# A two-layer hybrid encoder on one core: the beginning written out by hand, two DMA queues at both ends

## The chip, the core and the metric

The kernel runs on one NeuronCore of a Trainium2 chip. The core has TensorE (matrix products and transposes, into PSUM), VectorE, ScalarE (ACT in the profile) and GpSimd (POOL) for everything else, and SyncE (SP), which here only issues transfers. Each engine works through its own instructions in program order and waits on semaphores for the others; sixteen DMA engines move data between HBM and SBUF. The metric is the device time in microseconds of one execution, as the median over several runs.

## What is computed

The reference is a trunk of DEPTH = 2 layers over x of 256 tokens by 1024 channels, all in float32:

```python
h = rms_norm(x, norm_mix_g)
proj = h @ w_in                       # 1024 x 2304, split into nine parts of 256
# four branches: retention, pooling, neighbourhood attention, memory attention
up = jnp.einsum('bsnc,ncd->bsnd', branches, w_branch)
gates = jax.nn.sigmoid(h @ w_gate).reshape(b, s, N_BRANCH, dm)
x = x + jnp.einsum('bsnd,bsnd->bsd', gates, up) @ w_out
a, g = jnp.split(rms_norm(x, norm_ffn_g) @ w_ffn_in, 2, axis=-1)
x = x + (jax.nn.silu(a) * g) @ w_ffn_out
```

The products with the weights (w_in, w_gate, w_mem_kv, w_branch, w_out, w_ffn_in, w_ffn_out) are nearly all of the arithmetic.

## The kernel before

The 256 tokens are two tiles of 128, t = 0 and 1. The weights come in 272 *slots* of 128 x 1024 numbers (two rows of 128 input channels by 512 output channels, as a rule), in the order in which TensorE takes them. A slot is loaded into one of four buffers `raw` by a DMA (512 KB), and then split: ScalarE copies it, rounded to float32r, to `whi` (`split_hi`, line 272), and VectorE writes the rest, `raw - whi`, to `wlo` (`split_lo`, line 277). `split_lo` also calls `issue_dmas` (line 260), which has SP issue the loads of the slots whose buffers come free. The activations are split in the same way into hi and lo. One product of 128 x 128 by 128 x 512 is made of three: hi with `whi`, hi with `wlo`, lo with `whi`. A slot gives each token tile two such triples (`emit`, six products of TensorE), so both tiles take twelve.

Before the first product, x must be there with the channels on the partitions. Each half (512 channels) of each tile is transposed in four blocks by TensorE against an identity matrix, into a PSUM bank; ScalarE scales by the norm's gain and rounds to `hhi`, VectorE writes `hlo` (`half_norm`). What scales by the RMS comes after the products.

The order of all instructions is found while the program is built. A class `Clock` keeps an estimate in microseconds of when each engine gets to what it has been given. The main loop (from line 1020) lets the chains of small work go on whose operands should be there (`background`), splits weights when the engines have caught up (`pump`), and then emits the next slot of one of the tiles. For the beginning this means: SP issues all first loads, in the order x of tile 0 first half, identity with gains, slot 0, x of tile 1 first half, slot 1, the two second halves of x, slots 2 and 3 (lines 1003 to 1010); four chains `half_norm` wait for their halves of x; and while the estimate says that the first slot isn't ready, the loop gives TensorE products of zeros (`B<-w` in the profile), which keep it busy. At the end, `store` adds the last product to x in pieces of 256 columns and has SP issue a DMA for each.

Of the kernel before, what the change touches and what calls it, by code (L numbers as in the profile page):

```python
# [42 lines left out]
class Engine:  # L43
    """An engine of nc whose instructions are also entered in the clock."""
# [19 lines left out]
class Clock:  # L64
    """An estimate in microseconds of when each engine gets to what has been given to it:
    the small work is handed out when its operands should be there, so that no queue waits on it."""
# [81 lines left out]
def tile_encoder(ctx: ExitStack, tc: tile.TileContext, a: dict, out: bass.AP):  # L148
# [103 lines left out]
    state = {"dma": 0, "hi": 0, "lo": 0, "free": 0, "urgent": 0}  # L252
# [7 lines left out]
    def issue_dmas(n=NR):  # L260
        while state["dma"] < min(n_slots, state["lo"] + n):
            j = state["dma"]
            src, dims = slots[j]
            dst = shaped(RAW[j % NR], dims)
            if len(dims) == 2:
                nc.sync.dma_start(out=dst, in_=src)
            else:
                for k in range(dims[0]):
                    nc.sync.dma_start(out=dst[:, k], in_=src[:, k])
            state["dma"] += 1  # L270

    def split_hi():
        j = state["hi"]
        nc.scalar.copy(WHI[j % NS], RAW[j % NR])
        state["hi"] += 1
# [11 lines left out]
    def pump():  # L287
        """split weights when the engines have caught up, the sooner the fewer slots are ready"""
        window = WINDOW[max(0, min(state["lo"] - items[min(pos[0], len(items) - 1)]["j"], len(WINDOW) - 1))]
        if state["urgent"]:  # L290
            window = min(window, 0.8)
        for _ in range(2):
            j = state["lo"]
            if j < state["hi"] and soon(clock.at["DVE"], window) and soon(clock.last(clock.writes, WHI[j % NS])):
                split_lo()
            j = state["hi"]
            if (j < min(n_slots, state["free"] + NS, state["lo"] + NR) and soon(clock.at["ACT"], window)
                    and soon(clock.last(clock.writes, RAW[j % NR]))
                    and soon(max(clock.last(clock.reads, w[j % NS]) for w in (WHI, WLO)))):
                split_hi()  # L300
# [31 lines left out]
    def start(gen, *reads):  # L332
        """reads: PSUM banks that gen still reads, until it calls done()"""
        hold(*reads)
        chains.append([clock.now, gen])

    def until(step):
        """a chain goes on after what it has just given out (None), that much later (a number), or at a time"""
        return step[0] if isinstance(step, tuple) else clock.mark + (step or 0)

    def background():
        """let every chain go on whose last instructions should be through"""
# [39 lines left out]
    def scale_rows(out, in_, col):  # L382
        """out = in_ * col, on the engine that is free sooner"""
# [6 lines left out]
    def hi_lo(hi, lo, ps, bank, flag):  # L390
        """hi now, lo when hi is there, which ends the hold on bank"""
# [14 lines left out]
    def half_norm(src, t, c, act, gain, flag, bank, pre=None):  # L406
        """Half c of src (token-major) transposed, times gain (there a column), and split.
        What follows the products with it scales by one over the RMS (rms_chain)."""
# [22 lines left out]
    def rms_chain(src, rs, junk, flag, after=()):  # L431
        """rs = one over the RMS of each row of src"""
# [11 lines left out]
    def norm(t, flag, gain, rs, pre):  # L444
        """both halves of the norm of X[t]"""
# [7 lines left out]
    def head_norm(ps, dst, g, scale=None):  # L453
        """dst = ps (times scale, by row) scaled to unit RMS in groups of 64, g of them."""
# [78 lines left out]
    def to_heads(left, right, gains):  # L533
        """Token-major [tok, 256], both, to heads with the token in the free dimension, split for scores left^T right:
        LS has hi of a head on its 64 partitions and lo on the others, RS hi on both, and RL lo."""
# [36 lines left out]
    def scores(out, h, tok):  # L572
        """the scores of head h, for the tokens tok of left, with all of right"""
# [5 lines left out]
    def attention(l, v, branch, bias):  # L579
        """softmax(q k + bias) v for four heads, two at a time, to BHI/BLO[branch]."""  # L580
# [122 lines left out]
    def decay_chain(l):  # L703
        """exp(|i - j| log gamma): the lesser of d lg_fwd and -d lg_bwd, both of which are at most 0 on their side"""
# [17 lines left out]
    def prefetch_chain(l):  # L722
        """parameters, and what comes in once the layer's norms are through"""
# [33 lines left out]
    def log_sigmoid():  # L757
        """lg = log sigmoid of the 16 decays: min(x, 0) - log1p(exp(-|x|))."""
# [27 lines left out]
    def add(n_js, act, bank, nk, n=512, first=True, last=True, req=None, end=None, lag=1):  # L786
        """bank(t) (+)= act of tile t @ the weights of the next n_js slots; nk k-tiles.
        req: what has to be there; end(t): what follows; lag: slots by which tile 0 may lead here."""
# [53 lines left out]
    def hid_chain(l, j, t, ps):  # L842
        """silu(a) * g, token-major"""
# [19 lines left out]
    def store(t, blk):  # L863
        for c in range(blk * 512, blk * 512 + 512, 256):
            o = X[t][:, c:c + 256]
            nc.vector.tensor_add(o, o, A[2 * t + blk][:, c % 512:c % 512 + 256])
            nc.sync.dma_start(out=out[0, t * P:(t + 1) * P, c:c + 256], in_=o)

    def layer(l):
# [23 lines left out]
        for n, br in enumerate(BRANCHES):  # L893
            for blk in range(2):
# [3 lines left out]
                # the gates of the first branch lie around the memory's product  # L898
# [49 lines left out]
    def ready(t):  # L948
        """when the next slot of tile t can be taken"""
# [34 lines left out]
    def warm(*aps):  # L984
        """products of zeros, which keep TensorE at its full clock until aps are there"""
        while clock.now < max(clock.last(clock.writes, x) for x in aps):
            nc.tensor.matmul(B[0][:, 0:P], W[0][:, 0:P], W[0][:, P:2 * P], start=True, stop=True)
            clock.at["PE"] += 0.21 if clock.now < 6.2 else 0
# [6 lines left out]
    with tc.manual_schedule():  # L995
        nc.vector.memset(W[0][:, 0:P], 0.0)
        nc.vector.memset(mhalf, -0.5)
        def load_x(t, c):
            nc.sync.dma_start(out=X[t][:, HALVES[c]], in_=a["x"][0, t * P:(t + 1) * P, HALVES[c]])

        nc.scalar.activation(small[0], mhalf, AF.Square)
        clock.at["ACT"] += 1.2
        load_x(0, 0)
        nc.sync.dma_start(out=ident_gain, in_=a["ident_gain"])
        issue_dmas(1)
        load_x(1, 0)
        issue_dmas(2)
        load_x(0, 1)
        load_x(1, 1)
        issue_dmas()  # L1010
        for c in range(2):
            for t in range(NT):
                start(half_norm(X[t], t, c, act_h, GAIN[0][0], f"h{t}@0", (C[0], B[1], C[1], A[3])[2 * t + c]))
# [5 lines left out]
        assert base[0] == n_slots  # L1019
        while pos[1] < len(items) or chains:  # L1020
# [13 lines left out]
            else:  # L1034
                if pos[0] == 0:
                    nc.tensor.matmul(B[0][:, 0:P], W[0][:, 0:P], W[0][:, 0:P], start=True, stop=True)
                    continue
# [79 lines left out]
```

## Time and profile before

| | |
|---|---|
| median of 3 runs | 852.66 us |
| lowest, highest run | 850.24, 854.39 us |
| span of the profiled execution, first to last instruction | 850.4 us |
| that execution's own time | not recorded beside its span |
| TensorE (PE) busy | 840.0 us, 99% |
| VectorE (DVE), ScalarE (ACT) busy | 553.3 us, 469.6 us |
| moved by DMA | 152.86 MB, mean 180 GB/s |
| mean granted TensorE clock | 0.998 |

In the profile's lines a piece of work is named by its engine, its line and the tiles it writes and reads, out<-in. All instructions go through one helper, so nearly all have line L59 and are told apart by tiles: `hhi`, `hlo` are the activations of the first products, `whi`, `wlo` the split weights, `raw` the loaded ones, A, B and C banks of PSUM. The start of an instruction is in us from the start of the span. PE's busy time counts each product from its start to its modelled end, so two that follow one another overlap: a product of 512 columns shows 0.39 us and the next begins some 0.23 us after it. PEclk is the share of the full clock that TensorE was granted.

### The profile page before, as it was taken

Reading aid. Unit: us, or ns where it says so; the run is one execution under the profiler, and the core shown is the slowest. Engines: PE = TensorE matmul, PEld = TensorE weight load, DVE = VectorE, ACT = ScalarE, POOL = GpSimd, SP = SyncE. Lnnn points to the kernel's source line nnn. Section 1 sums busy time; section 2 is a strip of 40 time slices with the busy share of each in tenths; the row PEclk is TensorE's granted clock in tenths of the full one; section 3 lists DMA queues with packets and bytes.
Section 4 is the critical chain, followed back from the end, with each engine's and each line's share of the span. In section 5 each row is a group of like instructions: output and inputs, shape, how many; then the busy total and the mean of one; then the engine's idle time right before and its main releaser. Section 6 shows DMA issues by size and latency. Waiting matters only on the chain.

```text
span 850.4 us, 10796 instructions
## 1 busy us (share of the span) xinstructions
PE 840.0 (99%) x3934; PEld 678.6 (80%) x3934; DVE 553.3 (65%) x807; ACT 469.6 (55%) x722; POOL 28.6 (3%) x30
## 2 busy tenths in 40 slices
PE   8999999999999999999999999999999999999998
PEld 7887777778887888888888877777788878888886
DVE  5898776665667656555568778567665775665541
ACT  7867867444556444444469676664454654444430
POOL 0300100000000000000012001000000000000000
PEclk9999999999999999999999999999999999999999
DMA  8946764454558666665363567345554675656611
GB/s 267 315 131 202 246 201 132 131 191 160 191 169 259 188 196 187 186 188 186 96 218 121 173 216 250 134 124 182 165 170 131 190 252 183 190 181 192 193 53 50
DMA packets 103749, 152.86 MB, mean 180 GB/s; under 512 B 6416, under 2 KB 55312, under 8 KB 103696
## 3 DMA queue, kind: packets, MB, share of 16 engines
q1 hardware_dynamic: 103696, 152.17, 56.3%
q8 instruction: 31, 0.51, 0.2%
q14 instruction: 22, 0.18, 0.1%
HBM read 151.10 MB, written 1.05 MB: 179 GB/s over the span
## 4 chain that ended last, share of the span: by engine, by line
PE 94%; DMA 3%; DVE 1%; ACT 1%; SPq 0%; issue 0%; DVEq 0%; ACTq 0%
PE A L59 62%; PE B L59 27%; PE C L59 5%; DMA raw<-in_w_ffn_out 2%; DMA mem<-in_pool_a 1%; DVE wlo L59 1%; DMA x<-in_x 1%; ACT whi L59 1%; DVE w L59 0%; SPq L59 0%; DVE x L59 0%; DVEq L1113 0%; ACTq L59 0%
## 5 line engine op out<-in xcount | busy, mean ns | idle before, releaser
L59 DVE TENSOR_TENSOR wlo<-raw,whi 128x1024 fp32r<-128x1024 f32 (+1 forms) x275 | 329.9, 1211 | 183.6 <-ACT whi L59 182.7
L59 ACT CAST whi<-raw 128x1024 fp32r<-128x1024 f32 x272 | 284.3, 1051 | 221.2 <-PE A L59 102.1
L59 PE MATMUL A<-whi,hhi 128*128 128x512 f32 (+1 forms) x544 | 215.6, 396 | 0.1
L59 PE MATMUL A<-whi,hlo 128*128 128x512 f32 (+1 forms) x544 | 209.4, 385 | 0.0
L59 PE MATMUL A<-wlo,hhi 128*128 128x512 f32 (+1 forms) x544 | 209.0, 384 | 0.0
L59 PEld LDWEIGHTS A<-whi,hhi 128*128 128x128 f32 x544 | 102.4, 188 | 24.1 <-issue 5.5
L59 PEld LDWEIGHTS A<-whi,hlo 128*128 128x128 f32 x544 | 102.4, 188 | 21.2 <-DVE hlo L59 0.5
L59 PEld LDWEIGHTS A<-wlo,hhi 128*128 128x128 f32 x544 | 102.6, 189 | 17.9
L59 PE MATMUL B<-whi,hlo 128*128 128x512 f32 x288 | 112.3, 390 | 0.1
L59 PE MATMUL B<-whi,hhi 128*128 128x512 f32 x288 | 112.3, 390 | 0.0
L59 PE MATMUL B<-wlo,hhi 128*128 128x512 f32 x288 | 112.1, 389 | 0.0
L59 PE MATMUL A<-whi,bhi 128*128 128x512 f32 x272 | 109.2, 401 | 0.0
L59 PE MATMUL A<-whi,blo 128*128 128x512 f32 x272 | 106.3, 391 | 0.0
L59 PE MATMUL A<-wlo,bhi 128*128 128x512 f32 x272 | 106.1, 390 | 0.0
L59 PEld LDWEIGHTS B<-whi,hlo 128*128 128x128 f32 x288 | 54.0, 188 | 12.1 <-DVE hlo L59 0.9
L59 PEld LDWEIGHTS B<-wlo,hhi 128*128 128x128 f32 x288 | 54.1, 188 | 11.2
L59 PEld LDWEIGHTS B<-whi,hhi 128*128 128x128 f32 x288 | 54.1, 188 | 11.1
L59 PEld LDWEIGHTS A<-whi,bhi 128*128 128x128 f32 x272 | 51.1, 188 | 11.4 <-issue 0.8
L59 PEld LDWEIGHTS A<-whi,blo 128*128 128x128 f32 x272 | 51.0, 188 | 11.0
L59 PEld LDWEIGHTS A<-wlo,bhi 128*128 128x128 f32 x272 | 51.2, 188 | 9.7
L59 DVE SCALAR_TENSOR_TENSOR w<-B,rms,w 128x256 f32<-128x256 f32 x72 | 34.6, 482 | 3.9 <-ACT w L59 2.6
L59 ACT CAST bhi<-C 128x512 fp32r<-128x512 f32 x28 | 16.4, 587 | 35.2 <-PE C L59 35.1
(112 smaller groups left out, 614.9 us busy)
## 6 DMA issues: line engine op xcount, KB each, us to landing
raw<-in_w_ffn_in SPq DMA_DIRECT2D x176, 256.0 KB, 3.3
raw<-in_w_gate SPq DMA_DIRECT2D x64, 512.0 KB, 3.8
raw<-in_w_ffn_out SPq DMA_DIRECT2D x44, 512.0 KB, 4.0
raw<-in_w_in SPq DMA_DIRECT2D x36, 512.0 KB, 4.6
raw<-in_w_branch SPq DMA_DIRECT2D x16, 512.0 KB, 5.0
raw<-in_w_out SPq DMA_DIRECT2D x16, 512.0 KB, 4.1
raw<-in_w_mem_kv SPq DMA_DIRECT2D x8, 512.0 KB, 5.1
xn<-in_bias SPq DMA_DIRECT2D x4, 512.0 KB, 5.8
```

What stands on the lines that cost most here:

```text
L59: return f(*args, **kw)
```

## The change

Comments and document strings are taken out. Beyond that there are three parts.

The loads of the beginning: ScalarE's queue issues the identity with the gains and the first half of x of tile 1; SP's queue issues the first half of x of tile 0, slot 0 as two transfers of half a slot, slot 1, the second half of x of tile 0, slot 2, the second half of x of tile 1, slot 3.

The beginning of the program: a function `begin` gives out the first instructions in a fixed order, up to the split of slot 3, and the main loop goes on from there. While it runs, `pump` does nothing. x's first halves are handled in pairs of blocks with PSUM banks of their own, the second halves as four blocks. Slot 0 is rounded by ScalarE in two halves. Fifteen products of zeros stand at fixed places. The chains `half_norm` for the first norm are gone.

The end: of the two pieces of each store, the second is issued by ScalarE's queue.

```diff
-            if len(dims) == 2:
+            if len(dims) == 2 and j:
                 nc.sync.dma_start(out=dst, in_=src)
             else:
                 for k in range(dims[0]):
     def split_hi():
         j = state["hi"]
-        nc.scalar.copy(WHI[j % NS], RAW[j % NR])
+        for o in HALVES if j < 1 else [slice(None)]:
+            nc.scalar.copy(WHI[j % NS][:, o], RAW[j % NR][:, o])
...
+        if state["by_hand"]:
+            return
...
     def store(t, blk):
-        for c in range(blk * 512, blk * 512 + 512, 256):
+        for i, c in enumerate(range(blk * 512, blk * 512 + 512, 256)):
             o = X[t][:, c:c + 256]
             nc.vector.tensor_add(o, o, A[2 * t + blk][:, c % 512:c % 512 + 256])
-            nc.sync.dma_start(out=out[0, t * P:(t + 1) * P, c:c + 256], in_=o)
+            (nc.scalar if i else nc.sync).dma_start(out=out[0, t * P:(t + 1) * P, c:c + 256], in_=o)
...
+    def warm(n):
+
+        for _ in range(n):
+            nc.tensor.matmul(B[0][:, 0:P], W[0][:, 0:P], W[0][:, 0:P], start=True, stop=True)
+
+    def begin():
+
+        parts = {(0, 0): (C[0], (0, 1)), (0, 1): (B[1], (2, 3)), (1, 0): (C[1], (0, 1)), (1, 1): (A[3], (2, 3)),
+                 (0, 2): (C[0], (4, 5, 6, 7)), (1, 2): (C[1], (4, 5, 6, 7))}
+
+        def turn(t, *which):
+            for c in which:
+                bank, ks = parts[t, c]
+                for i, k in enumerate(ks):
+                    nc.tensor.transpose(bank[:, i * P:(i + 1) * P], X[t][:, k * P:(k + 1) * P], ident)
+
+        def split(t, c):
+            bank, ks = parts[t, c]
+            ks = [(bank[:, i * P:(i + 1) * P], GAIN[0][0][:, k:k + 1], *act_h(t, k)) for i, k in enumerate(ks)]
+            for ps, g, hi, lo in ks:
+                nc.scalar.activation(hi, ps, AF.Copy, scale=g)
+            for ps, g, hi, lo in ks:
+                nc.vector.scalar_tensor_tensor(out=lo, in0=ps, scalar=g, in1=hi.bitcast(F32), op0=ALU.mult, op1=ALU.subtract)
+            if c:
+                raise_flag(f"h{t}@0c{c - 1}")
+
+        def weights():
+            split_hi()
+            split_lo()
+
+        state["by_hand"] = True
+        warm(10)
+        turn(0, 0, 1)
+        warm(3)
+        split(0, 0)
+        weights()
+        turn(1, 0, 1)
+        warm(2)
+        split(1, 0)
+        emit(0)
+        split(0, 1)
+        emit(1)
+        weights()
+        split(1, 1)
+        turn(0, 2)
+        emit(0)
+        emit(1)
+        split(0, 2)
+        weights()
+        turn(1, 2)
+        split(1, 2)
+        weights()
+        state["by_hand"] = False
...
-        nc.scalar.activation(small[0], mhalf, AF.Square)
-        clock.at["ACT"] += 1.2
-        load_x(0, 0)
-        nc.sync.dma_start(out=ident_gain, in_=a["ident_gain"])
-        issue_dmas(1)
-        load_x(1, 0)
-        issue_dmas(2)
-        load_x(0, 1)
-        load_x(1, 1)
-        issue_dmas()
-        for c in range(2):
-            for t in range(NT):
-                start(half_norm(X[t], t, c, act_h, GAIN[0][0], f"h{t}@0", (C[0], B[1], C[1], A[3])[2 * t + c]))
+        nc.scalar.dma_start(out=ident_gain, in_=a["ident_gain"])
+        load_x(nc.sync, 0, 0)
+        load_x(nc.scalar, 1, 0)
+        nc.scalar.activation(small[0], mhalf, AF.Square)
+        clock.at["ACT"] += 1.2
+        issue_dmas(2)
+        load_x(nc.sync, 0, 1)
+        issue_dmas(3)
+        load_x(nc.sync, 1, 1)
+        issue_dmas()
...
         assert base[0] == n_slots
+        begin()
         while pos[1] < len(items) or chains:
...
-                if pos[0] == 0:
-                    nc.tensor.matmul(B[0][:, 0:P], W[0][:, 0:P], W[0][:, 0:P], start=True, stop=True)
-                    continue
```

More of the change, by code (lines that the diff above doesn't have):

```diff
@@ L251, in tile_encoder @@
     HALVES = [slice(c * 512, (c + 1) * 512) for c in range(2)]
-    state = {"dma": 0, "hi": 0, "lo": 0, "free": 0, "urgent": 0}
+    state = {"dma": 0, "hi": 0, "lo": 0, "free": 0, "urgent": 0, "by_hand": False}
     done_slots = set()
@@ L982, in emit @@
             it["end"](t)
[L984 to L988, printed above, removed]
+    def warm(n):
[44 more added lines that the diff above has]
+        state["by_hand"] = False
     def first_rms(t):
@@ L997, in tile_encoder, with load_x @@
         nc.vector.memset(mhalf, -0.5)
-        def load_x(t, c):
-            nc.sync.dma_start(out=X[t][:, HALVES[c]], in_=a["x"][0, t * P:(t + 1) * P, HALVES[c]])
+        def load_x(queue, t, c):
+            queue.dma_start(out=X[t][:, HALVES[c]], in_=a["x"][0, t * P:(t + 1) * P, HALVES[c]])
+        nc.scalar.dma_start(out=ident_gain, in_=a["ident_gain"])
+        load_x(nc.sync, 0, 0)
+        load_x(nc.scalar, 1, 0)
         nc.scalar.activation(small[0], mhalf, AF.Square)
         clock.at["ACT"] += 1.2
-        load_x(0, 0)
-        nc.sync.dma_start(out=ident_gain, in_=a["ident_gain"])
-        issue_dmas(1)
-        load_x(1, 0)
         issue_dmas(2)
-        load_x(0, 1)
-        load_x(1, 1)
+        load_x(nc.sync, 0, 1)
+        issue_dmas(3)
+        load_x(nc.sync, 1, 1)
         issue_dmas()
-        for c in range(2):
-            for t in range(NT):
-                start(half_norm(X[t], t, c, act_h, GAIN[0][0], f"h{t}@0", (C[0], B[1], C[1], A[3])[2 * t + c]))
         for t in range(NT):
```

## The prediction

> **What bounds the kernel now.** I read the page first, then the chain of waits over the first 40 us, then stages, DMA issues and single instructions of the beginning and the end.
>
> ```profile
> span 850.4 us, 10796 instructions
> PE 840.0 (99%) x3934; PEld 678.6 (80%) x3934; DVE 553.3 (65%) x807; ACT 469.6 (55%) x722; POOL 28.6 (3%) x30
> ```
>
> ```profile
> 2.12 5.63 DMA x<-in_x
> ...
> 7.80 1.12 PE C L59 x4
> 8.91 0.85 PE B L59 x4
> 9.77 1.28 PE A L59 x3
> 11.05 0.55 PE B L59 x4
> 11.59 19.55 PE A L59 x88
> ```
>
> ```profile
> 100.00:830.00 730.00, 726.90 (x3393) 586.22 (x3392) 471.44 (x640) 393.48 (x581) 16.38 (x17) 1.00 0.56 176
> ```
>
> TensorE sets the end. From 100 to 830 us it is idle for 730.00 - 726.90 = 3.1 us, so the change can win at the two ends and little in between. The chain says where the beginning goes: the first half of x for token tile 1 (x1a below; b is a second half) is issued at 2.12 us, fourth in SP's queue, and lands at 2.12 + 5.63 = 7.75. Its four transposes come at 7.80, four useless products (B<-w) stand behind them, three real products end at 11.05, and from about 11.4 TensorE runs without a gap (88 products in 19.55 us, 0.222 us each). The four useless products cost nothing: what they end at 9.4 is the wait for the split of the first weights (below).
>
> The loads of the beginning, by SP's issues, and then by the time from issue to landing, in the same order (x0a, the identity and gains, weight slots 0 and 1, x0b, x1b, slots 2 and 3; x1a is in the chain):
>
> ```profile
> 0.74 0.39 SPq L59 DMA_DIRECT2D x<-in_x  x1
> 1.18 0.41 SPq L59 DMA_DIRECT2D ident_gain<-in_ident_gain  x1
> 1.65 0.43 SPq L59 DMA_DIRECT2D raw<-in_w_in  x1
> 2.12 0.47 SPq L59 DMA_DIRECT2D x<-in_x  x1
> 2.63 0.43 SPq L59 DMA_DIRECT2D raw<-in_w_in  x1
> 3.10 1.17 SPq L59 DMA_DIRECT2D x<-in_x  x2
> 4.32 1.59 SPq L59 DMA_DIRECT2D raw<-in_w_in  x2
> ```
>
> ```profile
> x<-in_x SPq DMA_DIRECT2D x1, 256.0 KB, 2.8
> ident_gain<-in_ident_gain SPq DMA_DIRECT2D x1, 88.0 KB, 2.5
> raw<-in_w_in SPq DMA_DIRECT2D x1, 512.0 KB, 4.5
> raw<-in_w_in SPq DMA_DIRECT2D x1, 512.0 KB, 6.4
> x<-in_x SPq DMA_DIRECT2D x1, 256.0 KB, 6.6
> x<-in_x SPq DMA_DIRECT2D x1, 256.0 KB, 6.8
> raw<-in_w_in SPq DMA_DIRECT2D x1, 512.0 KB, 7.4
> raw<-in_w_in SPq DMA_DIRECT2D x1, 512.0 KB, 8.2
> ```
>
> Issue plus delay gives landings of 3.54, 3.68, 6.15, 7.75 (x1a), 9.0, 9.7, about 10.4, 11.7 and about 13.1 us. They come in the order of issue while issues wait in the engines, so the bytes decide: 344 KB are down by 3.68, 856 by 6.15, 1112 by 7.75, 1624 by 9.0, 1880 by 9.7, 2136 by 10.4, 2648 by 11.7.
>
> **The clock.** The stages between the third and the fourth wait:
>
> ```profile
> 4.32:7.73 3.41, 1.04 (x9) 0.85 (x7) 1.60 (x5) 2.18 (x5) 0.00 (x0) 1.00 0.96 312
> 7.70:8.40 0.70, 0.60 (x3) 0.60 (x4) 0.70 (x2) 0.00 (x0) 0.00 (x0) 0.52 1.07 413
> 8.40:10.80 2.40, 2.40 (x10) 2.05 (x9) 0.82 (x4) 1.85 (x5) 0.00 (x0) 0.50 1.05 401
> 10.80:11.30 0.50, 0.50 (x4) 0.45 (x3) 0.50 (x3) 0.23 (x1) 0.00 (x0) 0.66 1.06 410
> ```
>
> After a stretch of 3.41 us in which TensorE worked 1.04 us, the granted clock is halved from 7.73 to about 11.14 (0.52, 0.50, 0.66), another 3.41 us. Before 7.7 the rows say 1.00, but the filler products say otherwise:
>
> ```profile
> 1.05 2.93 PE L59 MATMUL B<-w 128*128 128x128 f32 x12 [1.05 <-DVE mhalf L59]
> 4.53 0.83 PE L59 MATMUL B<-w 128*128 128x128 f32 x6
> 4.73 1.14 ACT L59 ACTIVATE hhi<-C,ident_gain 128x128 fp32r<-128x128 f32 x4 [2.49 <-PE C L59]
> 5.90 1.13 DVE L59 SCALAR_TENSOR_TENSOR hlo<-C,ident_gain,hhi 128x128 fp32r<-128x128 f32 x4 [4.89 <-ACT hhi L59]
> 6.17 1.04 ACT L59 CAST whi<-raw 128x1024 fp32r<-128x1024 f32 x1 [0.30 <-DMA raw<-in_w_in]
> 7.25 1.29 DVE L59 TENSOR_TENSOR wlo<-raw,whi 128x512 fp32r<-128x512 f32 x2 [0.22 <-ACT whi L59]
> ```
>
> Twelve take 2.93 us at 1.05 and six 0.83 us at 4.53, 0.24 and 0.14 us for one. So the clock was half until about 4.3 and full from there to 7.7.
>
> **The change, part by part.** *Loads.* ACT now issues the identity with the gains (88 KB) and x1a; SP issues x0a, slot 0 in two halves, slot 1, x0b, slot 2, x1b, slot 3. No ACT issue stands in this trace; SP's cost 0.39 to 0.58 us, so I take 0.45 each, from about 0.74: x1a goes out near 1.2 instead of 2.12. ACT's table load and its first small instruction move back by 0.9, to about 3.1, before its first split. If the two queues share the engines evenly, x1a and slot 0's first half both end with 856 KB: 6.15 at the latest; x1a alone ahead would have 600 KB down at 3.68 + 2.47/2 = 4.9. Bounds for x1a 4.9 to 6.15, for the first half 5.0 to 6.15; I take 5.5 and 6.1. The second half is at 1112 KB: 7.75 as its upper end; on the line from 856 (6.15) to 1624 (9.0) 7.1; taken 7.4. Slot 1 has 1624, so 9.0 as before, x0b 9.7 as before, slot 2 (2392) 11.05 instead of 11.7, x1b (2648) 11.7 instead of 10.4.
>
> [...]
>
> *ACT by hand.* One split of 128x128 is 0.25 us apart from the next (four in 1.14), two take 0.62; half a slot is 0.55. First pair of x0a 4.3 to 4.9; slot 0 first half 6.1 to 6.7, second 7.4 to 8.0; x1a's first pair 8.6; second pair of x0a 9.1; slot 1 10.15; second pair of x1a 10.8; x0b's four after their transposes, 12.2; slot 2 13.2; x1b's four, behind their transposes, 15.2; slot 3 16.25. Each VectorE part follows it: low halves of slot 0 at 7.4 and 8.7, x1a 9.3, slot 1 at 10.9 and 11.5, second pair of x1a 12.1, slot 2 about 14.6, slot 3 about 17.4.
>
> *TensorE by hand.* Ten fillers at half clock end at 3.2, x0a's transposes near 4.6, three fillers 4.9, x1a's transposes near 6.0, two fillers. Tile 0 on slot 0 starts at 7.0 and is held by the second half's low part (8.7): end 9.1. Tile 1 on slot 0, six products of 0.222: 10.5. x0b's transposes (four in 0.55, by the chain) 11.05; tile 0 on slot 1 12.4; tile 1 on slot 1 13.7; x1b's transposes 14.3. What is queued behind each wait is all the rest of TensorE, since the order is fixed.
>
> *Sum.* At 14.3 us the new order has 24 products and all 16 transposes done. The kernel before has by then 3 products and 12 transposes from before 11.4, then 2.9 us less the last four transposes (0.55), which is 10.6 products: 13.6. The lead is 10.4 x 0.222 = 2.3 us. Late next is slot 3: its low part at 17.4 stands against TensorE's need at 14.3 + 2 x 6 x 0.222 = 17.0, so 0.4 is given back: 1.9 us. Bounds: with the loads at their late ends (second half 7.75) all of it comes 0.35 later, 1.5; with their early ends 0.3 earlier, 2.2. SP's later issues (slots 4 and 5) wait for the low parts of slots 0 and 1, at 8.7 and 11.5, against 8.54 and 12.45 in the trace, so no load is late; the small parameter loads now queue behind slot 4's wait, some 3 us after SP was free for them before (4.32 + 1.59 = 5.9), with their first use, after the first block of products (eight slot passes, so beyond 18 us), as cover. If that cover were gone, 3 us would show.
>
> *Stores.* The last:
>
> ```profile
> 846.59 0.75 DVE L59 TENSOR_TENSOR x<-x,A 128x256 f32<-128x256 f32 x2 [0.61 <-PE A L59]
> 847.04 0.33 SPq L59 DMA_DIRECT2D out<-x  x1
> 847.46 0.38 SPq L59 DMA_DIRECT2D out<-x  x1
> ```
>
> The second addition ends at 847.34, SP's first issue at 847.37, the second issue starts at 847.46. ACT, free there, could start at about 847.38: 0.1 us won. Bounds: 0.1 lost (a slower issue on ACT) to 0.12 won.
>
> The sum is 1.9 + 0.1 = 2.0 us, made against the profiled span: 850.4 - 2.0 = 848.4. No time of the profiled execution beside its span is given; the median of the runs, 852.66, lies 2.3 above that span, so I subtract from it: **850.7 us**.
>
> **Rivals.** (1) *The clock halves in the middle of the new beginning.* In the stretch 4.32 to 7.73 the new order works about 1.9 us by my list, against 1.04 that were not enough. If 1.9 isn't either, the stretch from 7.73 to 11.14 holds 3.41/2 = 1.7 us of full-clock work, where my list has 10 products and four transposes, 2.8 us: 1.1 lost. Gain 0.9: 851.8. For it: nothing in the trace shows what share suffices; against: TensorE's pauses are shorter. [...]
>
> (2) *The second queue does not bring x1a early.* If ACT's 1.28 us table load stays ahead of its issues (in the trace it starts at 0.73, ahead of everything), the identity lands at 2.0 + 2.5 = 4.5 and x1a near 2.5 + 5.6 = 8.1. All of TensorE stands behind x1a's transposes: 24 products (5.3 us) and 8 transposes (1.1 us) from 8.6 end at 15.0, not 14.3. Gain 1.3: 851.4. Where the load is put the code does not tell.
>
> (3) *ACT and VectorE do not follow.*
>
> ```profile
> 11.32:20.00 8.68, 8.68 (x43) 7.22 (x42) 7.02 (x18) 8.31 (x20) 1.11 (x2) 1.00 0.81 243
> 30.00:40.00 10.00, 10.00 (x52) 8.32 (x51) 8.99 (x23) 9.93 (x22) 4.66 (x5) 1.00 0.89 293
> ```
>
> ACT is busy 8.31 of 8.68 us and 9.93 of 10: no room to catch up. The RMS squares, which `first_rms` lets go once slot 2's high part is given out, now come behind slot 3's, since nothing runs between the two. If these engines pace TensorE there, all of the lead goes, and the stores are left: 852.6, no change. Against: they stay ahead of TensorE in the trace, which has no gap there.
>
> (4) *Slower: the plan behind the beginning turns out worse.* The rest is handed out by an estimated clock, whose state after the new beginning is another, so the order of small work and splits shifts through all layers. The 3.1 us of idle TensorE from 100 to 830 are such places. If they double, 2.0 won and 3.1 lost: 853.8. It decides from 2.0 us of new idle time on. For it: a long tail of decisions depends on that state; against: the same rules hold, and 3.1 us in 730 says they work well. The same lottery may win up to 3.
>
> **Chances.** Forecast 0.45; clock 0.15; no early x1a 0.08; supply 0.14; worse plan 0.13; a plan better by over 1.5 us 0.05. Against the median of 852.66, 0.5% (about what a measurement of this kernel can tell from no change) is 4.3 us: below 848.4 or above 856.9. Faster needs the forecast plus a better plan, or a good draw in the runs, which spread over 4 us: 0.10. Slower needs 6.2 us of new idle time, twice today's, or a bad draw with rival 4: 0.04. Same: 0.86. The range takes in rivals 1 to 3 and the near part of 4, with the runs' own spread on the fast side: 847.8 to 853.6.
>
> **What would show it.** Right: x1a's transposes before 6.5 us, the first real product near 7.0, no gap in TensorE from about 8.7, 24 products by about 14.3, a span shorter by about 2 us, idle time from 100 to 830 near 3 us. Wrong: x1a landing after 7; a granted clock of 0.50 where the first two slots run; TensorE waiting for low parts of weights between 15 and 40 us; new gaps in the layers.

## The result, and the profile after

The changed kernel takes 860.37 us (median of 4 runs, 859.57 to 861.12). The kernel before takes 852.4 us (median of 4 runs, 850.24 to 854.39; the run that came with its profile took 852.14). The ratio is 1.0106 [1.0089, 1.0123]: slower by about 8 us, where 850.7 us and "no change" had been forecast. In each of the two profiled executions the time is the span and about 1.75 us (860.47 and 858.7; 852.14 and 850.4), so the spans can be compared.

The page of the changed kernel:

```profile
span 858.7 us, 10821 instructions
PE 844.4 (98%) x3942; PEld 680.3 (79%) x3942; DVE 552.7 (64%) x804; ACT 479.2 (56%) x732; POOL 29.1 (3%) x30
```

ScalarE is busy 9.6 us longer and has ten instructions more. TensorE's 4.4 us more are in part products that ran at half the clock (0.63 us in place of 0.39 each), as shown below.

**The beginning itself went as forecast.** TensorE's instructions in the first microseconds (start, busy time, then operation, tiles and shapes; in brackets the idle time before):

```profile
1.05 4.31 PE L59 MATMUL B<-w 128*128 128x128 f32 x20 [1.05 <-DVE mhalf L59]
5.20 0.38 PE L59 MATMUL C<-ident_gain,x 128*128 128x128 f32 x2
...
6.31 0.38 PE L59 MATMUL C<-ident_gain,x 128*128 128x128 f32 x2
6.53 0.38 PE L59 MATMUL A<-ident_gain,x 128*128 128x128 f32 x2
...
7.11 0.47 PE L59 MATMUL A<-whi,hhi 128*128 128x512 f32 x1
...
8.75 0.50 PE L59 MATMUL A<-wlo,hhi 128*128 128x512 f32 x1 [0.23 <-DVE wlo L59]
```

The transposes of x1a come at 6.31 instead of 7.80, and the first product starts at 7.11.

**What comes behind it did not.** The same view from 14.0 us on:

```profile
14.02 0.49 PE L59 MATMUL C<-ident_gain,x 128*128 128x128 f32 x3
14.27 0.48 PE L59 MATMUL A<-whi,hhi 128*128 128x512 f32 x1
...
15.51 0.40 PE L59 MATMUL A<-whi,hlo 128*128 128x512 f32 x1
...
16.68 0.50 PE L59 MATMUL A<-whi,hhi 128*128 128x512 f32 x1 [0.77 <-ACT whi L59]
...
18.03 0.50 PE L59 MATMUL A<-wlo,hhi 128*128 128x512 f32 x1 [0.85 <-DVE wlo L59]
```

At 14.27 all transposes and 24 products are done. Tile 0 then takes slot 2 (six products, to 15.9) and at once slot 3, for whose high part it waits 0.77 us and for whose low part 0.85 us. In the kernel before, tile 1 takes slot 2 in between. A stretch of half clock follows. The windows view (window and its length; busy time and instructions of PE, PEld, DVE, ACT, POOL; granted clock, DMA share, GB/s):

```profile
15.12:18.53 3.41, 1.79 (x7) 0.95 (x6) 2.81 (x6) 3.41 (x7) 0.00 (x0) 1.00 0.54 157
18.53:21.94 3.41, 3.41 (x9) 2.67 (x9) 2.37 (x6) 3.35 (x9) 0.72 (x2) 0.50 0.78 228
...
117.52:120.93 3.41, 3.41 (x8) 2.61 (x9) 2.25 (x4) 2.70 (x6) 0.00 (x0) 0.50 0.51 154
```

Where the other idle time is, two windows of the layers tell, first of the kernel before, then of the changed one:

```profile
60.00:160.00 100.00, 99.48 (x481) 76.94 (x479) 75.15 (x116) 71.87 (x111) 2.93 (x2) 1.00 0.57 180
160.00:830.00 670.00, 667.42 (x3124) 541.47 (x3124) 428.23 (x580) 353.82 (x520) 16.16 (x16) 1.00 0.56 178
```

```profile
60.00:160.00 100.00, 94.16 (x450) 72.88 (x449) 68.22 (x109) 79.50 (x118) 2.35 (x2) 0.98 0.55 175
160.00:830.00 670.00, 668.25 (x3121) 540.90 (x3120) 433.75 (x587) 355.24 (x520) 16.16 (x16) 1.00 0.57 179
```

From 60 to 160 us TensorE's idle time goes from 0.52 to 5.84 us, and the clock is halved once more (117.52). From 160 on it is no worse: 1.75 us idle, against 2.58. In the bad stretch ScalarE is busier by 7.6 us, and the groups of instructions there name the reason (kernel before, then changed kernel, 60 to 160 us; count, busy time and mean, idle time before):

```profile
L59 ACT ACT_TABLE_LOAD x5 | 6.4, 1283 | 0.1
```

```profile
L59 ACT ACT_TABLE_LOAD x11 | 14.1, 1283 | 0.2
```

Over the whole span the changed kernel has 16 of these table loads, the kernel before 10. In the changed kernel's trace each but the first (at 1.66) stands between a sigmoid and the next exponential, or between an exponential and the next sigmoid. The new plan lets the two take turns. The chain of waits of the changed kernel between 78 and 91 us (start, length, what; the pieces named only "ACT L59" of 1.28 us are table loads):

```profile
83.53 1.28 ACT L59
...
84.83 1.10 ACT sc L59 x4
...
85.94 1.28 ACT L59
...
87.24 0.69 ACT gt L59
...
87.94 1.28 ACT L59
...
89.24 0.63 ACT mem L59
```

`sc` are the exponentials of an attention, `gt` the sigmoids of the gates. Meanwhile TensorE waits. The waits of the changed kernel in three windows, 78 to 91, 104 to 118 and 134 to 157 us (waiting engine and tile, what it waits for; us in total, times, longest):

```profile
PE B L59 <- ACT sc L59: 1.5, 1, 1.5
```

```profile
PE A L59 <- ACT gt L59: 2.0, 1, 2.0
```

```profile
PE B L59 <- DVE sc L59: 1.9, 1, 1.9
...
PE A L59 <- ACT gt L59: 0.4, 1, 0.4
```

To place the losses, the start of tile 1's first product on slot n was set against the same product of the kernel before (both profiled executions, us, negative is earlier). The one of the kernel before is the one of the prediction, with its stretch of half clock from 7.73 to 11.14; what that means for the lead comes further down:

```
slot              1      6     20     26     32     52     80    271
changed       -2.79  +1.50  +1.66  +3.38  +6.52  +9.42  +8.51  +8.38
```

The lead of 2.8 us (with some transposes still to come) is gone by slot 6: 1.6 us of waits for slot 3, another 1.6 to 1.7 of half clock, and 1.1 which includes those transposes. Between slots 20 and 52 another 7.8 us go: 1.5 + 2.0 + 1.9 + 0.4 = 5.8 of waits and 3.41/2 = 1.7 of half clock account for 7.5.

### The profile page after: what moved, and what is told of

Its sections match the earlier page's. It is cut to its first block, busy times and chain, and to the rows that moved or that the text cites. A ratio compares the mean times of both kernels' runs of the same rounds, so it can differ in the third digit from the quotient of the medians.

```text
span 858.7 us, 10821 instructions
## 1 busy us (share of the span) xinstructions
PE 844.4 (98%) x3942; PEld 680.3 (79%) x3942; DVE 552.7 (64%) x804; ACT 479.2 (56%) x732; POOL 29.1 (3%) x30
## 3 DMA queue, kind: packets, MB, share of 16 engines
HBM read 151.10 MB, written 1.05 MB: 177 GB/s over the span
## 4 chain that ended last, share of the span: by engine, by line
PE 88%; ACT 4%; DMA 3%; DVE 2%; issue 1%; SPq 0%; DVEq 0%; ACTq 0%
PE A L59 57%; PE B L59 27%; PE C L59 4%; DVE wlo L59 1%; DMA raw<-in_w_ffn_out 1%; DMA raw<-in_w_gate 1%; ACT whi L59 1%; ACT L59 1%; DMA raw<-in_w_in 1%; ACT sc L59 0%; ACT gt L59 0%; ACT rs L59 0%; DVE w L59 0%; ACT pt L59 0%; ACT ls L59 0%
## 5 line engine op out<-in xcount | busy, mean ns | idle before, releaser
L59 DVE TENSOR_TENSOR wlo<-raw,whi 128x1024 fp32r<-128x1024 f32 (+1 forms) x275 | 330.0, 1211 | 186.8 <-ACT whi L59 186.0
L59 ACT CAST whi<-raw 128x1024 fp32r<-128x1024 f32 (+1 forms) x273 | 284.0, 1048 | 214.0 <-PE A L59 96.5
L59 PE MATMUL A<-whi,hhi 128*128 128x512 f32 (+1 forms) x544 | 216.2, 397 | 0.9 <-ACT whi L59 0.8
L59 PE MATMUL A<-wlo,hhi 128*128 128x512 f32 (+1 forms) x544 | 209.7, 385 | 1.1 <-DVE wlo L59 1.1
L59 PE MATMUL A<-whi,hlo 128*128 128x512 f32 (+1 forms) x544 | 209.8, 386 | 0.0
L59 PEld LDWEIGHTS A<-whi,hhi 128*128 128x128 f32 x544 | 102.6, 189 | 25.2 <-issue 4.9
L59 PEld LDWEIGHTS A<-whi,hlo 128*128 128x128 f32 x544 | 102.7, 189 | 21.3 <-DVE hlo L59 0.5
L59 PEld LDWEIGHTS A<-wlo,hhi 128*128 128x128 f32 x544 | 102.9, 189 | 19.9 <-DVE wlo L59 2.0
L59 PE MATMUL A<-whi,bhi 128*128 128x512 f32 x272 | 110.0, 405 | 2.5 <-ACT gt L59 2.5
L59 PE MATMUL B<-whi,hlo 128*128 128x512 f32 x288 | 112.3, 390 | 0.1
L59 PE MATMUL B<-whi,hhi 128*128 128x512 f32 x288 | 112.3, 390 | 0.0
L59 PE MATMUL B<-wlo,hhi 128*128 128x512 f32 x288 | 112.1, 389 | 0.0
L59 PE MATMUL A<-whi,blo 128*128 128x512 f32 x272 | 106.8, 393 | 0.0
L59 PE MATMUL A<-wlo,bhi 128*128 128x512 f32 x272 | 106.5, 392 | 0.0
L59 PEld LDWEIGHTS B<-whi,hlo 128*128 128x128 f32 x288 | 54.1, 188 | 12.1 <-DVE hlo L59 0.9
L59 PEld LDWEIGHTS A<-whi,bhi 128*128 128x128 f32 x272 | 51.5, 189 | 15.1 <-ACT gt L59 3.3
L59 PEld LDWEIGHTS B<-wlo,hhi 128*128 128x128 f32 x288 | 54.1, 188 | 11.2
L59 PEld LDWEIGHTS B<-whi,hhi 128*128 128x128 f32 x288 | 54.1, 188 | 11.1
L59 PEld LDWEIGHTS A<-whi,blo 128*128 128x128 f32 x272 | 51.3, 189 | 11.2
L59 PEld LDWEIGHTS A<-wlo,bhi 128*128 128x128 f32 x272 | 51.6, 190 | 9.8
L59 DVE SCALAR_TENSOR_TENSOR w<-B,rms,w 128x256 f32<-128x256 f32 x72 | 34.6, 482 | 3.9 <-ACT w L59 2.6
L59 ACT CAST bhi<-C 128x512 fp32r<-128x512 f32 x28 | 16.4, 586 | 35.3 <-PE C L59 35.1
```

Source lines behind the costliest of these rows:

```text
L59: return f(*args, **kw)
```

## The experiments

Two theories stood against each other first. *Table loads*: the plan's new order makes ScalarE switch tables more often, and this costs most of the time. *Order and supply*: slot 3 before its time and the shifted splits cost it, and the table loads lie under cover. Ratios are to runs of the kernel before on the same chip.

**The same two kernels without table switches.**

```diff
-        nc.scalar.activation(g, ps, AF.Sigmoid, scale=RH[t])
+        nc.scalar.activation(g, ps, AF.Copy, scale=RH[t])
```

(and the two other sigmoids). The estimated clock costs both functions alike, so the order of the instructions stays. The results are then not the reference's, since the sigmoids are left out. First the changed kernel:

> The kernel after, with every sigmoid on ScalarE replaced by a plain scaled copy, so that ScalarE never has to load another function table after the first one (the gates and the SwiGLU are computed without their sigmoid). The order of all instructions stays that of the kernel after. Theory P (the plan behind the beginning): the beginning itself wins its 2 us; of the 8.3 us that the profiled span grew, the six more table loads of 1.28 us (16 against 10) cost the four waits of TensorE between 88 and 157 us, 1.5 + 2.0 + 1.9 + 0.4 = 5.8, and the half clock from 117.5 to 120.9, 1.7. Expected 860.4 - 7.5 = 852.9, ratio to the kernel before 0.999 to 1.002. Rival S (the beginning, its two queues or the splits cost the time; table loads are covered by other work): 1.009 to 1.011 as the kernel after.

Measured 851.84 us, 1.0014 [0.9999, 1.0029]. The same edit on the kernel before:

> The kernel before with the same replacement (no sigmoid, one table load in all). Theory P: its ten table loads stand where TensorE shows no wait over 0.5 us, so 0 to 1 us faster: ratio 0.999 to 1.000. Rival S: 1.000. If table loads cost the same everywhere, nine loads of 1.28 us would give 11.5 us: 0.9865.

Measured 851.39 us, 1.0002 [0.9986, 1.0018]. The switches cost the kernel before nothing that can be measured; the changed one is 0.9% faster without them, a part of which is the half clock behind slot 3, absent in this trace (below). Along the slots, against the kernel before:

```
slot                      1      6     20     32     52    271
changed, copies       -2.79  -0.09  +0.10  +0.16  +0.09  +0.12
```

So the rise between slots 20 and 52 was all table loads and what follows on them. Its first 20 us repeat the order and the waits of the changed kernel, without the half clock. TensorE's two waits in this kernel, and its clock behind them:

```profile
16.69 0.50 PE L59 MATMUL A<-whi,hhi 128*128 128x512 f32 x1 [0.77 <-ACT whi L59]
18.05 0.50 PE L59 MATMUL A<-wlo,hhi 128*128 128x512 f32 x1 [0.86 <-DVE wlo L59]
```

```profile
18.53:22.00 3.47, 3.47 (x17) 2.85 (x16) 2.38 (x6) 3.41 (x9) 0.77 (x2) 1.00 0.80 233
```

At slot 6 the two kernels are 1.59 us apart: the price of one stretch of half clock. That stretch stands ahead of every switch in the layers, so it isn't their price: four of the ten runs of this kernel have a mean granted clock of 0.996 to 0.998, the other six 1.000, so it seems to come in some executions and not in others. Even so the beginning wins nothing here (+0.12 at the end): of the 2.7 us of lead lost by slot 6, 1.6 are the waits for slot 3, and the rest includes the transposes still to come.

**Why tile 0 takes slot 3 too early.** The plan lets a tile take a slot when the flag of its half of x is due. `raise_flag` sets that time to `clock.mark`, which is moved up to the end of every operation given out, loads of weights too, and is set back only where a chain of small work goes on or a block of products ends. `begin` has neither before its last flag; so the flag of x1b isn't due before the last load given out has landed in the estimate. The theory: set back, tile 1 takes slot 2 in time, and the lead stays.

```diff
         def split(t, c):
+            clock.mark = clock.now
```

> The kernel after with one line more: before each split of x by hand the estimate's mark is set to TensorE's time, so that the flag of tile 1's second half no longer carries the landing time of a weight load. The plan then gives tile 1 slot 2 right after tile 0, before slot 3, and has 12 table loads instead of 16. Theory P: the wait of 1.6 us at 15.5 to 18.0 and the half clock behind it (1.7) go, and about two thirds of the loss to table loads: 860.4 - 3.4 - 5 = 852, ratio 0.997 to 1.001. Rival S: 1.007 to 1.011.

Measured 854.19 us, 1.0032 [1.0018, 1.0046], outside what was expected. The first half of the theory holds. The stage after the beginning has 0.49 us of idle TensorE in place of 1.62:

```profile
14.27:18.53 4.26, 3.77 (x17) 2.67 (x16) 3.38 (x7) 4.26 (x9) 0.00 (x0) 1.00 0.51 162
60.00:160.00 100.00, 96.75 (x458) 74.58 (x457) 71.82 (x112) 74.50 (x112) 2.94 (x2) 1.00 0.56 179
```

The second row says where the lead goes instead in the profiled execution, the fastest of the ten: 3.25 us idle in the layers, most of it in one wait near 99 us (seven of the ten have a granted clock of 0.997 or 0.998, against 1.000 here, so the median of 854.19 holds a half clock besides, which this trace can't place):

```profile
PE C L59 <- DVE w L59: 3.1, 1, 3.1
```

This order has 12 table loads, not 16. A pause of the estimate behind the beginning draws other orders from the same plan. With 1.0 and with 1.25 us, below, TensorE takes the slots in the same order to the end; what differs is the small work between them:

```diff
         state["by_hand"] = False
+        clock.at["PE"] += 1.0
```

> The same, and TensorE's estimated time is put on by 1.0 us where the work by hand ends, which gives a plan with 10 table loads, as many as the kernel before has. Theory P: the whole lead of the beginning is left, 2 to 2.5 us: 850.2, ratio 0.996 to 0.999. Rival S: 1.007 to 1.011.

Measured 852.92 us, 1.0020 [1.0007, 1.0034], outside what was expected. The same with 1.25 in place of 1.0:

> The kernel with the mark set and TensorE's estimated time put on by 1.25 instead of 1.0 us. The same beginning, and the first 14 slot passes in the same order as with 1.0, but the plan behind has 16 table loads instead of 10. Theory P: the waits around 75 to 130 us of the kernel after come back, 4 to 8 us over the variant with 1.0 (852.9): 857 to 861, ratio 1.007 to 1.011. Rival S or N: as with 1.0, 1.002.

Measured 863.46 us, 1.0130 [1.0108, 1.0153], above the 1.007 to 1.011 expected. A quarter of a microsecond in an estimate makes a difference of 1.1%. The table loads of the two (1.0, then 1.25) over the whole span, and their windows in the layers:

```profile
L59 ACT ACT_TABLE_LOAD x10 | 12.8, 1283 | 1.8 <-PEq L1155 1.7
```

```profile
L59 ACT ACT_TABLE_LOAD x16 | 20.5, 1283 | 1.9 <-PEq L1155 1.7
```

```profile
60.00:160.00 100.00, 99.33 (x476) 76.72 (x475) 75.49 (x122) 71.72 (x113) 2.94 (x2) 1.00 0.56 180
```

```profile
60.00:160.00 100.00, 93.78 (x442) 72.75 (x441) 66.89 (x105) 78.16 (x118) 3.00 (x2) 0.97 0.55 173
```

Ten loads leave 0.67 us of idle TensorE there, sixteen 6.22 and a lower clock. That the order with ten is still slower than the kernel before (1.0020) is not the tables': between 14.3 and 60 us TensorE is idle for 2.19 us there, 1.0 of it in one wait at 37 us, where the kernel before has no gap.

**Is the wait at 99 us a table matter too?** Both edits together, the mark set back and copies in place of the sigmoids:

> The kernel with the mark set (plan with tile 1's slot 2 in its place), and all sigmoids replaced by a scaled copy, so that there is one table load. Theory P: the lead of 1.9 us that the kernel with the sigmoids showed until 90 us stays if what came at 99 us there (a wait of 3.1 us) hangs on table loads: 849.5, ratio 0.998. If that wait is another (a weight load that the plan issues late), it stays: 1.002.

Measured 850.35 us, 0.9983 [0.9970, 0.9996]. The wait is 0.6 us instead of 3.1, and a lead is left at the end:

```
slot                      1      6     20     32     52    271
mark                  -3.20  -1.89  -2.01  +1.55  +1.54  +0.01
mark, copies          -2.79  -1.45  -0.86  -0.72  -0.74  -1.74
```

So the kernel with the new beginning is about 1.4 us (0.17%) faster where the plan behind it does no harm.

**What the 1.4 us are.** The tables so far set the new beginning against one execution of the kernel before, in which the clock was halved from 7.73 to 11.14. The two rewritten versions of the kernel before, with copies (above) and with tanh (below), have its order on TensorE, and their times don't differ from its own. In their profiled executions the granted clock is not halved there (in the one with copies the first products still start 0.43 us apart, at half pace, until about 10.3; in the one with tanh they start 0.23 apart from 8.7 on). The stretch in the one with tanh:

```profile
7.73:11.14 3.41, 3.19 (x23) 2.54 (x22) 2.76 (x8) 2.88 (x9) 0.00 (x0) 1.00 1.05 396
```

The spans of the kernel before and of the new beginning with its mark, first with copies, then with tanh:

```profile
span 848.9 us, 10787 instructions
span 848.6 us, 10805 instructions
```

```profile
span 849.0 us, 10795 instructions
span 848.5 us, 10811 instructions
```

Slot by slot, each against the kernel before with the same rewriting:

```
slot                      1      6     10     20     52    271
mark, copies          -2.14  -0.81  -0.12  -0.11  +0.02  -0.29
mark, tanh            -1.05  +0.29  +0.33  +0.23  +0.35  -0.43
```

Here the lead is spent by slot 10, and 0.3 to 0.5 us are won in the whole span, instead of 1.8 to 1.9 against the execution with the half clock (850.4). The runs say the same. Of the 99 runs of the kernel before that stand beside the experiments (a hundredth, of 2140 us, is left aside), 34 have a mean granted clock of 0.998 or less (one halved stretch of 3.41 us in 850 takes 0.002 off the mean); of the 22 runs of the two versions, mark with copies and mark with tanh, none has. Runs with 0.999 or more alone have medians of 850.84 and 850.96 for the kernel before and of 850.35 for both versions, so 0.5 to 0.6 us is left. More than half of what the new beginning wins is therefore a half clock that it avoids; the rest, by these traces, comes between slot 52 and the end, and whether the beginning or only the plan makes it is not shown.

**The new beginning in front of the old order.** If the forecast's lead of 2.3 us is real, the kernel before's recorded order from slot 2 on, with its table loads and its stores, should keep it; the rival is that splits and RMS squares in that order stand where the earlier TensorE runs into them.

```diff
+        head, rest = RECORD[:START[0]], RECORD[START[0]:]
...
+        for e in rest:
+            call(e)
```

`RECORD` holds the instructions of the kernel before in its order, `START` the place of the first product of slot 2; ahead of `rest` stand the new loads and the new beginning.

> The new beginning (loads by two queues, fillers, transposes, splits and the first 24 products by hand, as in the kernel after), and behind it every instruction in the order that the kernel before has, recorded from its own plan, from the first product of slot 2 on; the stores as before. Theory P (the plan behind the beginning costs the time, the beginning wins): ten table loads at their old places, no wait for slot 3 ahead of tile 1's slot 2, so the lead of the beginning stays to the end: 1.5 to 2.3 us faster than the kernel before, ratio 0.9973 to 0.9985. Rival S (the beginning or its second queue costs time): 1.000 or above. Rival N (the lead is eaten by ScalarE and VectorE behind the beginning, whatever the plan): 0.9995 to 1.001.

Measured 851.89 us, 1.0003 [0.9992, 1.0014]: the rival. Its waits between 16 and 22 us:

```profile
PE A L1063 <- DVE wlo L1063: 1.4, 2, 0.8
PE A L1063 <- ACT whi L1063: 0.7, 1, 0.7
```

They are for slots 3 and 4, whose splits stand on ScalarE behind RMS squares. Then those four squares were moved behind the high parts of slots 3, 4 and 5, the small work that follows them behind the low part of slot 5, and slot 3 was split in halves:

```diff
+            if slot_of(e[5], WHI, 7) == [6] and squares:
+                for q in squares:
+                    call(q)
...
+                for o in HALVES:
+                    r.scalar.copy(WHI[3][:, o], RAW[3][:, o])
```

> As the kernel with the new beginning and the old order behind it, but the four RMS squares of ScalarE, which stood ahead of the splits of slots 3 and 4 there, come behind those of slots 3, 4 and 5 (VectorE's and GpSimd's small steps with them behind the low part of slot 5), and slot 3 is split in halves. In the trace of the kernel without this, TensorE waits 0.72 + 0.75 us for slot 3 and 0.66 for slot 4 between 16.9 and 21.6 us, 2.1 in all. Theory: these waits were what ate the lead, so 1.5 to 2 us come back: ratio 0.9975 to 0.999 to the kernel before. Rival: the lead meets another limit of ScalarE and VectorE a few slots on (slots 6 to 10), and the ratio stays at 1.000.

Measured 851.42 us, 1.0002 [0.9993, 1.0011]. The waits only move: 0.10 us at 19.0, 0.35 at 27.8, 0.41 at 34.9, 0.90 at 100.4. So three orders behind the new beginning that have no more table loads than the kernel before (this one, the one it starts from, and the pause of 1.0) are none of them faster than that kernel. None of the 24 runs with the old order behind the new beginning has a granted clock under 0.999, so they avoid the half clock too; against the runs of the kernel before with 0.999 or more (medians 850.62 and 850.84) their medians of 851.89 and 851.42 are 1.3 and 0.6 us slower.

**The loads and the stores by themselves.** The changed kernel with all first loads on SP's queue in their old order, slot 0 whole:

```diff
-        nc.scalar.dma_start(out=ident_gain, in_=a["ident_gain"])
-        load_x(nc.sync, 0, 0)
-        load_x(nc.scalar, 1, 0)
+        load_x(0, 0)
+        nc.sync.dma_start(out=ident_gain, in_=a["ident_gain"])
```

> The kernel after with the loads of the kernel before (all by SP's queue in the old order, slot 0 in one transfer); the order on every engine is otherwise that of the kernel after, table loads included. Tells what the second queue and the halves do. Theory P: x1a lands at 7.75 instead of about 6.2 and TensorE's order waits for it, so the first two slots come about 1.5 us later; the wait of 1.6 us at 15.5 for slot 3 swallows up to that, since ScalarE is what sets it: 860.4 to 862, ratio 1.010 to 1.013. If the second queue itself costs time (rival S): under 1.009.

Measured 862.06 us, 1.0115 [1.0091, 1.0139]. TensorE waits for x1a, and the first product comes 1.06 us later than in the changed kernel:

```profile
7.31 0.44 PE L59 MATMUL C<-ident_gain,x 128*128 128x128 f32 x2 [0.71 <-DMA x<-in_x]
...
8.17 0.48 PE L59 MATMUL A<-whi,hhi 128*128 128x512 f32 x1
```

By slot 1 only 0.31 us of that is left (-2.48 against -2.79), by slot 6 0.32 (+1.82 against +1.50). So in these two traces the order by hand gives nearly all of the lead, the second queue and the halves 0.3 us. (x1a lands at 5.9 us instead of 7.2, which is more than the 0.9 between its issue times; but its place among the loads changed too, so the run does not separate queue from order.) The kernel before with the new stores alone:

```diff
-            nc.sync.dma_start(out=out[0, t * P:(t + 1) * P, c:c + 256], in_=o)
+            (nc.scalar if i else nc.sync).dma_start(out=out[0, t * P:(t + 1) * P, c:c + 256], in_=o)
```

> The kernel before with the change of the last stores alone (the second piece of each by ScalarE's queue). All theories: between 0.12 won and 0.1 lost, not to be told from no change, 0.999 to 1.001; the last transfer starts near 0.04 us after the last addition instead of 0.12.

Measured 851.6 us, 0.9995 [0.9983, 1.0007]: no difference that can be told. The last DMA is issued 0.03 us after the last addition instead of 0.12.

**A version with fewer switches.** With sigmoid(x) = (1 + tanh(x/2))/2 the gates take tanh. The products with the gate become (t - 1)·x on VectorE with t = tanh(-x/2), and the factor -0.5 goes into a scale that follows; the mark is set back as above. The sigmoids of the SwiGLU stay.

```diff
-        nc.scalar.activation(g, ps, AF.Sigmoid, scale=RH[t])
+        nc.scalar.activation(g, ps, AF.Tanh, scale=rhalf[:, t:t + 1])
...
-            nc.vector.tensor_mul(m, ps, g)
+            less_one(m, g, ps)
```

> A whole kernel again: the new beginning with the mark set, and the sigmoids of the branch gates and of the retention gate written as 0.5 (1 - tanh(-x/2)), whose function stands in the same table as the exponential (four table loads instead of 12; the instruction order on TensorE is that of the variant with the copies). The factor -0.5 is taken up where the merged branches are split, and one small GpSimd step a token tile and layer gives minus half of one over the RMS. Theory P (the beginning wins, the table loads of the plan behind it lose): as the variant with the copies, 0.9983, less what VectorE's slightly dearer instructions cost: 0.998 to 0.9995. Rival: the other waits of this plan (99 us) come back: 1.000 to 1.002.

Measured 850.35 us, 0.9986 [0.9975, 0.9996], and 1.2% under the changed kernel's 860.37. It has four table loads:

```profile
L59 ACT ACT_TABLE_LOAD x4 | 5.1, 1283 | 2.4 <-PEq L1174 1.7 <-PE B L59 0.7
```

```profile
60.00:160.00 100.00, 99.39 (x479) 76.70 (x478) 75.09 (x117) 66.34 (x107) 2.94 (x2) 1.00 0.57 180
```

The rewrite alone, on the kernel before:

> The kernel before with the same rewriting of the gates (four table loads instead of ten) and its own beginning. Theory P: its table loads stood under cover, so nothing changes: 0.9995 to 1.0005. If the loads cost something there too, it gains as much as the variant above and the new beginning is worth nothing: 0.998 to 0.999.

Measured 851.45 us, 0.9996 [0.9983, 1.0009]. The tables are worth nothing there, as with the copies; so the gain of the version before comes with the beginning, mostly as the half clock that it avoids, and the rewrite keeps the plan from spending it.

## Why the prediction was wrong

**The beginning of the changed kernel: right.** x1a was put at 5.5 us; issued at 1.175, it took 4.7, so 5.9. The first product was put at 7.0 and came at 7.11; 24 products by 14.3, and they were done at 14.27. The fillers were mis-sized: "twelve" in the row of before are records, and a filler product of 128 x 128 in float32 leaves two, so the ten (x20 above) end at 5.2, not 3.2. That held x0a's transposes back by 0.6 us to 5.20; the first product was hardly later for it.

**Slot 3: the first step that failed.** The sum gave back 0.4 us because slot 3's low part, at 17.4, was set against a need at 14.3 + 2 x 6 x 0.222 = 17.0. This took it that both tiles take slot 2 first. The plan had tile 0 go on to slot 3, whose high part TensorE wanted at about 15.9 and got at 16.68, and the low part at 18.0: 1.6 us instead of 0.4. The order is in the code (a mark that `begin` doesn't set back) and was not worked out. That setting the mark back mends it is shown; the 0.49 us left near there are close to the 0.4 forecast.

**Rival 4, and the step that cost most: table loads were put at nothing.** The rival had the right direction, and the wrong price and place. It named the plan's new order as the danger, and 3.1 us of idle time from 100 to 830 us that might double. But the wide window hid what decides. The loss is in 80 to 156 us alone, 7.8 us from slot 20 to 52, and its price isn't read from the idle time of before, which was small just because five table loads lay under cover there. Each further one puts 1.28 us on ScalarE, ahead of a result or a split that TensorE waits for. Table loads were not in the sum, though the groups of instructions of before had them: ten, of 1.283 us each. That they and their consequences make up this loss is shown by the copies: the same order without them gains and loses nothing between slots 20 and 52 (+0.10 to +0.09, where the changed kernel goes from +1.66 to +9.42). The three orders from one plan with 12, 10 and 16 loads (1.0032, 1.0020, 1.0130) fit that, but differ in other waits too.

How often the tables were loaded went with the functions and their order: 16 times in the changed kernel, 12 with the mark set back, 4 with tanh in place of the gates' sigmoids besides, and once with the mark set back and copies in place of all sigmoids. A load took 1283 ns in each of these, and beside the eleven from 60 to 160 us of the changed kernel ScalarE was idle for 0.2 us in all, 0.02 for one.

**Rival 1, the clock: right in kind, wrong in place.** In the stretch from 4.32 to 7.73 TensorE was busy for all 3.41 us, not for 1.9, since the fillers took twice their forecast, and no halving followed; the halvings came at 18.53, behind the waits for slot 3 (1.62 us), and at 117.52, behind that for `gt` (2.03). One costs 1.6 to 1.7 us. So in this execution nearly as much again was lost behind each of these waits, which the price of rival 4 left out. That TensorE's work in one stretch sets the clock of the next was the author's estimate from the one halving of before (1.04 of 3.41 us busy ahead of it); the traces do not settle it (last section).

**Rival 2: did not happen.** ScalarE's table load came at 1.66 us, after its DMA issues (0.73 and 1.18). **Rival 3: not as the first limit, but as the next.** With the old order behind the new beginning, and with the RMS squares out of the way, waits for the work of ScalarE and VectorE took the lead away (1.0003, 1.0002). Which engine would have to become faster to keep it was not tried.

**The stores** were put at 0.1 us; issue to addition moved by 0.09, and the time can't tell it.

**The sum itself: the lead was mis-sized.** The 2.3 us were counted against one execution of the kernel before, and the half clock from 7.73 to 11.14 in it was taken as part of that kernel. It is not in every execution: against the two profiled ones without it, of the rewritten versions in the same order, the new beginning leads by 2.1 us (copies) and 1.05 us (tanh) at slot 1, where the execution that the prediction read gives 2.8, and all of it is spent by slot 10. With the plan's harm taken out, the runs gain 1.4 and 1.2 us (0.9983, mark and copies; 0.9986, mark and tanh), with 0.3 to 2.6 in the interval of the first; 0.5 to 0.6 is left where no clock was halved. The forecast's 2.0 thus lies within the interval, but not as the lead that it was added up from. The base was off as well: 852.66 was the median of three runs, and the later sets of 22 to 31 runs have 851.1 to 851.4. What failed besides was the chance of 0.04 for slower: a program whose order hangs on an estimated clock was treated as if its rows beyond 60 us would stay nearly the same.

## What to carry to other kernels

Where a planner orders the program by cost estimates, an edit in one place is an edit everywhere behind it: compare the order of instructions on each engine, before any time, and look first for costs that the planner doesn't count, here the table switches of ScalarE (1.28 us each). Price an extra wait not only at its length but with the half clock that may follow it (here 1.6 to 1.7 us behind waits of 1.6 and 2.0 us, and none behind the same 1.6 in the trace with copies), and ask of a gain whether it is a half clock that the profiled execution of the old kernel happened to have: the granted clock of every run tells. Take away the cause of such a cost (here with tanh in the gates, 4 table loads instead of 12) before judging the edit itself, since the draw of the plan (1.002 to 1.013 for 0.25 us in an estimate) is larger than the edit (0.998).

## What was unexpected of the hardware

The share of busy time does not tell in these traces when the clock is halved. The two halvings of the changed kernel each last 3.41 us and start 98.99 us apart, 29 times that length. If the clock was set in stretches of that length all along, which these two numbers suggest and do not show, the stretches lie as in what follows. After the stretch from 15.12 to 18.53, with TensorE busy 1.79 of 3.41 us (0.52), the next was halved. Before the halving at 117.52 stand two stretches, and the last of them was busy 2.96 of 3.42 us:

```profile
110.69:114.10 3.41, 1.84 (x9) 1.18 (x7) 2.27 (x3) 3.35 (x5) 0.00 (x0) 1.00 0.68 192
114.10:117.52 3.42, 2.96 (x11) 1.86 (x11) 2.16 (x3) 3.42 (x5) 0.00 (x0) 1.00 0.19 71
```

That 2.96 misleads, since the ends of products are modelled: eight of these eleven products have 256 columns and most of them start some 0.31 us apart, where products of 512 columns start 0.23 apart elsewhere. Counted at 0.23 us for 512 columns (an estimate from these starts), the stretch before the second halving holds 1.6 us of work (0.47), and the one before the first, with five products, 1.1 us (0.33). The stretch from 110.69 has seven products of 512, 1.6 us as well, and was not followed by a halving, so whether a share of work decides, and which, stays open.

The changed kernel with copies had the same two waits, 0.77 and 0.86 us, and kept the full clock; where its stretches begin is not seen in its trace, as none is halved near there, so that they lie otherwise there is only a guess at the reason. The kernel before has its halving from 7.73 in one trace, from 8.41 in the one with the new stores, and none in its two rewritten versions, so where a halved stretch lies, if there is one, differs between executions. What decided here was not settled.
